# A spacer of 448 bytes, value products in two runs and query turns of 128 columns in a hybrid attention trunk

## The chip, the cores and the metric

The kernel runs on one core of a Trainium2 chip. The metric is device time in microseconds of one execution, as the median of several runs. TensorE (PE in the rows) does the matmuls and, in a queue of its own (PEld), loads the stationary operand; VectorE is DVE, ScalarE is ACT, GpSimd is POOL, and SyncE (SP) issues the transfers.

## The reference, cut to what matters

Two layers act on 1024 latent and 256 context tokens of width 1024. In each, a normalised input goes through one input projection and from there into three parallel mixers (a spatial gating MLP, a windowed attention with 8 query and 2 key heads, a linear recurrence), whose outputs meet in one output projection; then comes a gated FFN of width 2816. The attention, to which most of the change belongs:

```python
s_loc = jnp.einsum('bnqhgd,bnkhd->bnhgqk', qb, kw).astype(jnp.float32) * scale
s_ctx = jnp.einsum('bnqhgd,bchd->bnhgqc', qb, kc).astype(jnp.float32) * scale
...
p = jax.nn.softmax(jnp.concatenate([sink_l, s_ctx, s_loc], axis=-1), axis=-1)
...
o = jnp.einsum('bnhgqc,bchd->bnqhgd', p_ctx, vc) + jnp.einsum('bnhgqk,bnkhd->bnqhgd', p_loc, vw)
```

A query tile of 128 tokens sees the two context tiles and up to three latent tiles, so it has 2 (context queries), 4 (the first and the last latent tile) or 5 key tiles. The FFN is `(silu(gu[..., :D_FF]) * gu[..., D_FF:]) @ w_down` with `gu = h @ w_gu`.

## The kernel before, in words

**Memory.** SBUF is cut into four pools in this order: constants, the weight pool (`wts`), small statistics (`stats`, from `small`), and 33 equal slots of 128 x 1280 float32 (5120 bytes of each partition) that `alloc` hands out and `rel` takes back in turn. Every large tile that isn't a weight lies in a slot: the activations `h`, `q` and `qs`, `P`, `PT`, `Vt`, `ah` and `al`. The weight buffers are 4096 bytes each and start at byte 25344 of a partition, the slots at byte 59712. Some weights of the out-projection and one pair of the FFN are put in slots too; in the rows they are `wsh` and `wsl` instead of `wh` and `wl`.

**Matmuls.** `mm` (L145) issues one, and so every matmul has line 145. `mm3` makes a product of two numbers that are each split in a high and a low part: high by high, high by low, low by high, as three matmuls. In the rows `dd<-h,wh` reads: output tile `dd` in PSUM, moving operand `h`, stationary operand `wh`; `128*128` is the part of the array that is used (rows by columns), and `128x512` is the moving operand. Operands of type float32 (in transposes and in `pv`) leave two rows per matmul where the others leave one; transposes of P and q come as four rows for a group of four by the names of this trace.

**Attention.** A unit is a query tile and one of two head groups: 20 units in layer 0 and 16 in layer 1. Four generators work at once on different units: `q_proj(n+2)` projects the queries (24 matmuls `mm<-wh,h` and `mm<-wl,h`), `a_q(n+1)` turns them (four transposes by the identity in `cst_sb`) and splits them into `qs`, `a_s(n)` computes scores (`dd<-kh,qs`, `dd<-kl,qs`) and the softmax `P`, and `a_o(n-1)` turns each 128 x 128 block of `P` and multiplies it by the values. A string of letters says whose turn it is, step by step (one step is the code up to the next `yield`):

```python
for z in "spspspspqopopsopopooos":
```

Between the steps a background list puts in small matmuls of the next stage (`xx<-jT`, 32 x 32). In `a_o` the turned blocks of key tile j go to PSUM, are copied to `PT` by ScalarE (even j, L1144) or VectorE (odd j, L1146), and `pv(j)` multiplies them: two matmuls `xx<-PT,Vt`, one for each half of the output partitions, with 64 stationary columns. Before the change pv(j-2) follows the transposes of block j, and the last two come one step apart after all blocks.

**FFN.** For each of 22 slices of 128 channels `gate_up` makes gate and up (`dd<-h,wh`: h moves, the weights are stationary) in groups of 512 or 256 tokens, and `ffn_down` adds the product with `w_down` (`mm<-wh,ah` and `xx<-wh,ah`: the weights move in 512 columns, the activation is stationary).

Of the kernel before, what the change touches and what calls it, by code (L numbers as in the profile page):

```python
# [10 lines left out]
F32 = mybir.dt.float32  # L11
# [80 lines left out]
def trunk(ctx: ExitStack, tc: tile.TileContext, x, ctxt, cc, w_mod, pp, w_in, w_out, lng, lnb, sgw, sink,  # L92
          w2, a2, g2, w_gu, w_down, cst, rope, out, dbg=None):
    nc = tc.nc
    V, S, G, T, D = nc.vector, nc.scalar, nc.gpsimd, nc.tensor, nc.sync
# [3 lines left out]
    stp = ctx.enter_context(tc.tile_pool(name="stats", bufs=4))  # L99
# [10 lines left out]
    def alloc(name, dt=F32):  # L110
        i = free.popleft()
        return Slot(sp.tile([128, NTOK], dt, tag=f"s{i}", name=nm(name)), i)

    def rel(*ss):
        for s in ss:
            free.append(s.i)
# [13 lines left out]
    def mm_t():  # L130
        return p_t("gg", 1) if psum["units"] else p_t("mm", 2)

    def x_t():
        return p_t("gg", 1) if psum["units"] else p_t("xx", 2)
# [9 lines left out]
    def mm(o, lhsT, rhs, start=True, stop=True):  # L144
        T.matmul(o, lhsT=lhsT, rhs=rhs, start=start, stop=stop)  # L145

    def mm3(o, a, b, start, stop):
        mm(o, a[0], b[0], start, False)
        mm(o, a[0], b[1], False, False)
        mm(o, a[1], b[0], False, stop)  # L150


    K = cp.tile([128, CSTW], F32, name="cst_sb")
    PP = cp.tile([128, L * PPW], F32, name="pp_sb")
    cs_ = alloc("silu")
# [2 lines left out]
    D.dma_start(PP, pp)  # L158
    ident = K[:, C_ID:C_ID + 128]
    blk = K[:, C_BLK:C_BLK + 128]  # L160
    mLK = K[:, C_LK:C_LK + 128]
    mG = K[:, C_G:C_G + 128]
    mF = K[:, C_F:C_F + 64]
    I2 = K[:, C_I2:C_I2 + 64]
    hs = K[:, C_HS:C_HS + 2]
# [68 lines left out]
    def wget(ahead=2, slots=False):  # L234
        if not ready:
            emit_w(slots)
        r = ready.popleft()
        while len(ready) < ahead and plan:
            emit_w(slots)
        return r  # L240
# [212 lines left out]
    def hk(hT, k, c0, n):  # L453
        if c0 < 256:
            return tuple(hT[z][k].t[:, 1024 + c0:1024 + c0 + n] for z in range(2))
        z = 0 if c0 >= 768 else 1
        o = c0 - (768 if z == 0 else 256)
        return tuple(hT[z][k].t[:, o + j:o + j + n] for j in (0, 512))
# [98 lines left out]
    def layer(l):  # L557
# [345 lines left out]
        for name in ("v", "u"):  # L903
# [3 lines left out]
            for t0 in range(0 if full else 2, NT, 2):  # L907
                ps = mm_t()
# [56 lines left out]
        def rot(ps, o, nh, n, tmp):  # L965

            hv = [128, nh, 64]
            v3 = lambda ap: ap.rearrange("p (h d) -> p h d", d=64)
            V.tensor_tensor(v3(o), v3(ps), rt4[:, 0, n:n + 1, :].to_broadcast(hv), op=ALU.mult)
            V.tensor_tensor(v3(tmp), v3(ps), rt4[:, 1, n:n + 1, :].to_broadcast(hv), op=ALU.mult)  # L970
            v4 = lambda ap: ap.rearrange("p (a b f) -> p a b f", b=2, f=16)
            G.tensor_tensor(v4(o), v4(o), v4(tmp)[:, :, ::-1, :], op=ALU.add)
# [5 lines left out]
        for t0 in range(0, NT, 2):  # L978
            ps = mm_t()
            for j in range(2):  # L980
                proj256((wA, wB), t0 + j, ps[:, j * 256:(j + 1) * 256])
            pv = ps.rearrange("p (j c) -> p j c", j=2)
# [45 lines left out]
        def a_geo(t):  # L1028
            if t < 2:
                return 0, 0, [0, 1]  # L1030
            lo = max(2, t - 1)
            hi = min(NT - 1, t + 1)
            return lo * 128, (hi - lo + 1) * 128, list(range(lo, hi + 1)) + [0, 1]
# [2 lines left out]
        wq, sst = {}, {}  # L1036
        QQ, QS = alloc("q"), alloc("qs", F32R)

        def q_proj(n):
            t, g = units[n]  # L1040
            if t == tiles_q[0]:
                wq[0] = wget(), wget()
            ps = mm_t()
            for k in range(8):
                wt = wq[0][k // 4]
                c = (k % 4) * 256
                mm3(ps[:, 0:256], hk(hT, k, t * 128, 128), (wt[0][:, c:c + 256], wt[1][:, c:c + 256]), k == 0, k == 7)
                if k < 7:
                    yield
            q = QQ.t[:, n % 2 * 640:n % 2 * 640 + 512]  # L1050
            if t < 2:
                S.activation(q[:, 0:256], ps[:, 0:256], AF.Copy)
            else:
                rot(ps[:, 0:256], q[:, 0:256], 4, t - 2, q[:, 256:512])

        def a_q(n):
            q = QQ.t[:, n % 2 * 640:n % 2 * 640 + 512]
            ps = x_t()
            for h in range(4):
                T.transpose(ps[0:64, h * 128:(h + 1) * 128], q[:, h * 64:(h + 1) * 64], ident)  # L1060
            s = QS.t[:, n % 2 * 640:n % 2 * 640 + 512]
            S.activation(s[0:64], ps[0:64, :], AF.Copy)
            V.tensor_tensor(s[64:128], ps[0:64, :], s[0:64].bitcast(F32), op=ALU.subtract)
# [55 lines left out]
        def a_o(n):  # L1119

            t, g = units[n]
            keys = a_geo(t)[2]
            P = sst.pop(n)
            PT = []
            po = x_t()

            def pv(j):
                for e in range(2):
                    c = (j % 2) * 512 + e * 256
                    mm(po[64 * e:64 * e + 64, 0:256], Vt.t[:, keys[j] * 128 + g * 64:keys[j] * 128 + g * 64 + 64],  # L1130
                       PT[j // 2].t[:, c:c + 256], j == 0, j == len(keys) - 1)
                if j % 2 or j == len(keys) - 1:
                    rel(PT[j // 2])
            for j in range(len(keys)):
                ps = x_t() if j % 2 else mm_t()
                for i in range(4):
                    c = (i % 2) * 640 + j * 128
                    z = (i % 2) * 2 + i // 2
                    T.transpose(ps[:, z * 128:(z + 1) * 128], P[i // 2].t[:, c:c + 128], ident)
                if j % 2 == 0:  # L1140
                    PT.append(alloc("PT"))
                o = PT[j // 2].t[:, (j % 2) * 512:(j % 2) * 512 + 512]
                if j % 2 == 0:
                    S.activation(o, ps, AF.Copy)  # L1144
                else:
                    V.tensor_copy(o, ps)  # L1146
                if j == len(keys) - 1:
                    rel(*P)
                if j >= 2:
                    pv(j - 2)  # L1150
                yield
            pv(len(keys) - 2)
            yield
            pv(len(keys) - 1)
            yield
            ot = alloc("attO")
            S.activation(ot.t[:, 0:256], po[:, 0:256], AF.Copy)
            D.dma_start(od[t][:, 256 + g * 256:512 + g * 256], ot.t[:, 0:256])
            rel(ot)
# [197 lines left out]

        N = len(units)
        weave(q_proj(0), k_turn(0))
        run(q_proj(1))  # L1360
        a_q(0)
        bs_ = beta_start()
        for n in range(N + 1):
            gs = {"s": a_s(n) if n < N else iter(()), "o": a_o(n - 1) if n else iter(()),
                  "p": q_proj(n + 2) if n + 2 < N else bs_}
            for z in "spspspspqopopsopopooos":
                if z != "q":
                    next(gs[z], None)
                elif n + 1 < N:
                    a_q(n + 1)  # L1370
            if n == N // 2 - 2:
                bgq.appendleft(k_turn(1))
            bg(BG_A)
            bg(EL_A, 1)
            if n == N // 2 - 2:
                while len(khh) < 2 or not rw.get('kt'):
                    bg(1)
            for z in "pos" if n + 2 < N or n == N else "os":
                run(gs[z])
            if n == N - 3:  # L1380
                rel(rt, *hT[0], *hT[1])
# [295 lines left out]
    for l in range(L):  # L1677
        layer(l)
# [33 lines left out]
```

## Time and profile before

| what | value |
|---|---|
| median of 3 runs | 3435.76 us (3434.49 to 3438.95) |
| the profiled execution | 3435.06 us |
| its span in the trace | 3433.3 us |
| TensorE busy | 3310.5 us (96%) |
| VectorE, ScalarE, GpSimd busy | 1789.0, 1256.5, 331.6 us (52%, 37%, 10%) |

The span is the time from the first to the last record; the execution's own time is 1.8 us longer. Busy shares are means over the program. Layer 0 has its attention at 376 to 585 us and its FFN at 950 to 1870 us; layer 1 has them at 2203 to 2400 and 2690 to 3433 us.

### The profile page before, as it was taken

The numbers are of one execution on the slowest core, as the hardware profiler recorded it, in microseconds if no ns is written. First come the engines' busy times: TensorE is split into PE (matmuls) and PEld (weight loads), VectorE is DVE, ScalarE is ACT, GpSimd is POOL, SyncE is SP. The second block draws the span as 40 slices with busy tenths as digits, with TensorE's granted clock in tenths as the row PEclk, the third lists the DMA queues.
The fourth block names the chain that finished last, engine by engine and source line by source line (L and its number), as shares of the span: only waits on it lengthen the run. The fifth ranks groups of instructions, "written<-read, shape, count | busy, mean of one in ns | idle before, by whom it ended". The sixth has DMA issues, their size and how long they took to land. (4 is left out here: it accounts for less than half of the span.)

```text
span 3433.3 us, 51729 instructions
## 1 busy us (share of the span) xinstructions
PE 3310.5 (96%) x20348; PEld 2646.9 (77%) x20348; DVE 1789.0 (52%) x3747; ACT 1256.5 (37%) x2735; POOL 331.6 (10%) x460
## 2 busy tenths in 40 slices
PE   7998999999999999999999998999999999999998
PEld 4777877777787777778888777877777788888887
DVE  3458778775523333333334658878674433433445
ACT  4354476663431111111113554466663411111112
POOL 2103101231100000000001202111121000000000
PEclk9998999999999999999999998999999999999999
DMA  5784212546312222221113375323445111111113
GB/s 205 235 251 141 76 59 68 141 135 221 130 46 72 80 86 80 73 69 62 37 37 107 110 236 162 114 63 89 111 143 190 56 43 44 49 49 50 49 41 119
DMA packets 381779, 354.40 MB, mean 103 GB/s; under 512 B 111968, under 2 KB 332768, under 8 KB 381536
## 3 DMA queue, kind: packets, MB, share of 16 engines
q1 hardware_dynamic: 381536, 351.09, 32.7%
q8 instruction: 161, 2.64, 0.3%
q14 instruction: 82, 0.67, 0.1%
HBM read 255.20 MB, written 95.81 MB: 102 GB/s over the span
## 5 line engine op out<-in xcount | busy, mean ns | idle before, releaser
L145 PE MATMUL dd<-h,wh 128*128 128x512 f32 (+1 forms) x3440 | 992.3, 373 | 2.6 <-DVE h L436 2.3
L145 PEld LDWEIGHTS dd<-h,wh 128*128 128x128 f32 x3440 | 624.8, 189 | 147.0 <-issue 30.2
L145 PE MATMUL dd<-h,wl 128*128 128x512 f32 (+1 forms) x1720 | 637.7, 371 | 0.0
L228 ACT ACTIVATE wh<-wr 128x1024 fp32r<-128x1024 f32 x172 | 180.7, 1058 | 694.3 <-PE xx L145 379.1
L229 DVE TENSOR_TENSOR wl<-wr,wh 128x1024 fp32r<-128x1024 f32 x172 | 209.4, 1225 | 348.6 <-ACT wh L228 344.1
L145 PEld LDWEIGHTS dd<-h,wl 128*128 128x128 f32 x1720 | 325.0, 189 | 62.9 <-issue 5.0
L145 PE MATMUL mm<-wh,h 128*128 128x256 f32 x1472 | 320.6, 295 | 1.9 <-ACT gel L913 1.4
L1514 DVE SCALAR_TENSOR_TENSOR ft<-ft,dd 128x512 f32<-128x512 f32 (+1 forms) x110 | 69.5, 632 | 459.6 <-ACT ft L1513 459.6
L145 PEld LDWEIGHTS mm<-wh,h 128*128 128x128 f32 x1472 | 247.7, 194 | 29.2 <-issue 26.5
L1513 ACT ACTIVATE ft<-dd 128x512 f32<-128x512 f32 (+1 forms) x110 | 60.5, 550 | 502.2 <-PE dd L145 501.6
L145 PE MATMUL mm<-h,wh 128*128 128x512 f32 (+1 forms) x816 | 234.6, 372 | 1.5 <-ACT ntmp L428 0.7
L176 POOL TENSOR_TENSOR ss<-ss,mh_sb 128x1 f32<-128x1 f32 x74 | 50.4, 682 | 1856.7 <-DVE ss L405 1850.4
L145 PE MATMUL mm<-wl,h 128*128 128x256 f32 x736 | 211.0, 287 | 4.9 <-DVE wl L229 4.9
L145 PEld LDWEIGHTS mm<-h,wh 128*128 128x128 f32 x816 | 145.5, 193 | 35.5 <-issue 10.8
L1545 DVE TENSOR_TENSOR yac<-yac,mm 128x512 f32<-128x512 f32 x180 | 123.4, 686 | 95.0 <-PE mm L145 94.8
L1545 DVE TENSOR_TENSOR yac<-yac,xx 128x512 f32<-128x512 f32 x180 | 123.5, 686 | 90.0 <-PE xx L145 90.0
L145 PE MATMUL mm<-wh,ah 128*128 128x512 f32 x396 | 157.1, 397 | 1.9 <-DVE yac L1545 1.8
L145 PE MATMUL xx<-wh,ah 128*128 128x512 f32 x396 | 157.0, 396 | 0.0
L145 PE MATMUL xx<-wl,ah 128*128 128x512 f32 x396 | 156.7, 396 | 0.0
L145 PE MATMUL mm<-wh,al 128*128 128x512 f32 x396 | 156.5, 395 | 0.0
L145 PE MATMUL xx<-wh,al 128*128 128x512 f32 x396 | 156.5, 395 | 0.0
L145 PE MATMUL mm<-wl,ah 128*128 128x512 f32 x396 | 156.5, 395 | 0.0
(315 smaller groups left out, 5965.8 us busy)
## 6 DMA issues: line engine op xcount, KB each, us to landing
wr<-in_w_gu SPq DMA_DIRECT2D x88, 512.0 KB, 3.7
wm<-in_w_mod SPq DMA_DIRECT2D x80, 512.0 KB, 4.5
wr<-in_w_down SPq DMA_DIRECT2D x44, 512.0 KB, 3.3
wr<-in_w_in SPq DMA_DIRECT2D x38, 512.0 KB, 4.8
cb<-ao SPq DMA_DIRECT2D x76, 256.0 KB, 3.0
ao<-rk SPq DMA_DIRECT2D x58, 256.0 KB, 4.1
xs<-xr SPq DMA_DIRECT2D x28, 512.0 KB, 2.8
xr<-xs SPq DMA_DIRECT2D x26, 512.0 KB, 4.3
```

Source lines behind the costliest of these rows:

```text
L145: T.matmul(o, lhsT=lhsT, rhs=rhs, start=start, stop=stop)
L176: G.tensor_tensor(dst, src, mh[:, :n], op=ALU.pow)
L228: S.activation(hi, raw, AF.Copy)
L229: V.tensor_tensor(lo, raw, hi.bitcast(F32), op=ALU.subtract)
L1513: S.activation(tm, ps[:, 0:n], AF.Tanh, scale=0.5)
L1514: V.scalar_tensor_tensor(tm, tm, 1.0, ps[:, 0:n], op0=ALU.add, op1=ALU.mult)
L1545: V.tensor_tensor(yac[t].t[:, c], yac[t].t[:, c], ps, op=ALU.add)
```

## The change

It has four edits. A tile of 112 float32 (448 bytes) that nobody uses is put at the start of the stats pool, so that every later tile of this pool and all slots start 448 bytes further: the slots at byte 60160 instead of 59712, the weights where they were. Per layer, two strips of 64 columns in the q tile are cleared on GpSimd. `a_q` turns 128 columns at a time, the head and what lies behind it, onto 128 partitions of PSUM, of which the upper 64 are not read; the cleared strip is what lies behind the last head of a unit. And `a_o` multiplies in two runs: for five key tiles pv(0) and pv(1) behind the transposes of block 3 and the rest behind the last block, one step later; for four or two key tiles all of them there.

```diff
+    stp.tile([128, 112], F32, name="gap", bufs=1)
     K = cp.tile([128, CSTW], F32, name="cst_sb")
...
         QQ, QS = alloc("q"), alloc("qs", F32R)
 
+        for z in range(2):
+            G.memset(QQ.t[:, z * 640 + 256:z * 640 + 320], 0.0)
+
         def q_proj(n):
...
             for h in range(4):
-                T.transpose(ps[0:64, h * 128:(h + 1) * 128], q[:, h * 64:(h + 1) * 64], ident)
+                T.transpose(ps[:, h * 128:(h + 1) * 128], q[:, h * 64:h * 64 + 128], ident)
...
                 if j == len(keys) - 1:
                     rel(*P)
-                if j >= 2:
-                    pv(j - 2)
+                if j == 3 and len(keys) == 5:
+                    pv(0)
+                    pv(1)
                 yield
-            pv(len(keys) - 2)
-            yield
-            pv(len(keys) - 1)
+            yield
+            for j in range(2 if len(keys) == 5 else 0, len(keys)):
+                pv(j)
             yield
```

The lines behind the first edit are numbered one higher after the change, those behind the second four higher. The diff doesn't show what the engines' orders become, so here are three pieces of them.

TensorE in the attention of layer 0, a unit with five key tiles, before; `mm<-cst_sb,P` and `xx<-cst_sb,P` are transposes of P, two from each of its two tiles, and a row with x2 behind `PT,Vt` is one key tile:

```order
L1139 MATMUL mm_4069<-cst_sb,P_3838 128x128 x2
L145 MATMUL xx_4038<-PT_4044,Vt_3013 64x256 x2
...
L1139 MATMUL xx_4081<-cst_sb,P_3838 128x128 x2
L145 MATMUL xx_4038<-PT_4044,Vt_3013 64x256 x2
...
L145 MATMUL xx_4114<-jT_3705 32x32 x13
...
L1139 MATMUL mm_4095<-cst_sb,P_3838 128x128 x2
L145 MATMUL xx_4038<-PT_4074,Vt_3013 64x256 x4
L145 MATMUL xx_4114<-jT_3705 32x32 x7
L145 MATMUL dd_4178<-kh_3434,qs_3417 128x256
L145 MATMUL xx_4038<-PT_4100,Vt_3013 64x256 x2
```

The same unit in the changed kernel:

```order
L1143 MATMUL mm_4072<-cst_sb,P_3841 128x128 x2
L145 MATMUL mm_4003<-wh_3010,h_234 128x256
...
L1143 MATMUL xx_4082<-cst_sb,P_3841 128x128 x2
L145 MATMUL xx_4041<-PT_4047,Vt_3014 64x256 x4
...
L145 MATMUL xx_4117<-jT_3708 32x32 x17
...
L1143 MATMUL mm_4098<-cst_sb,P_3841 128x128 x2
L145 MATMUL xx_4041<-PT_4077,Vt_3014 64x256 x4
L145 MATMUL xx_4117<-jT_3708 32x32 x3
L145 MATMUL dd_4181<-kh_3437,qs_3418 128x384
L145 MATMUL dd_4181<-kh_3437,qs_3418 128x256
L145 MATMUL xx_4041<-PT_4103,Vt_3014 64x256 x2
```

Four runs of pv became three: the first two key tiles now go together behind the fourth block. Over both layers TensorE's order has 115 runs of these matmuls before and 75 after, with 320 matmuls in both.

GpSimd in layer 0, from the gating MLP (`gel`) to the attention, after the change; `q` is the tile whose strips are cleared, `kt` the keys whose rotation GpSimd finishes:

```order
L916 TENSOR_SCALAR gel_2994<-gel_2994 128x512
L1041 MEMSET q_3417 128x64 x2
L973 TENSOR_TENSOR kt_3015<-kt_3015,rtmp_3149 128x128 x2
L973 TENSOR_TENSOR kt_3015<-kt_3015,rtmp_3251 128x128 x2
L973 TENSOR_TENSOR kt_3015<-kt_3015,rtmp_3343 128x128 x2
```

The two clears were not there before; the rest is in the same order.

## Rows read from the trace of the kernel before

**Rows 1.** Windows: stretch, length, busy us of each engine, granted clock, DMA share, GB/s.

```profile
376.00:585.00 209.00, 205.85 (x1931) 165.96 (x1929) 167.05 (x464) 144.31 (x334) 25.42 (x44) 1.00 0.22 62
...
2360.00:2400.00 40.00, 33.77 (x312) 23.36 (x306) 32.34 (x90) 27.83 (x60) 7.48 (x15) 1.00 0.39 119
```

**Rows 2.** Timeline of TensorE, attention of layer 0: start, length, operation.

```profile
417.59 0.60 PE L1139 MATMUL xx<-cst_sb,P 128*128 128x128 f32 x4
417.94 0.37 PE L145 MATMUL mm<-wh,h 128*128 128x256 f32 x1
...
418.38 0.60 PE L1139 MATMUL mm<-cst_sb,P 128*128 128x128 f32 x4
418.91 0.65 PE L145 MATMUL xx<-PT,Vt 128*64 128x256 f32 x4
419.49 0.38 PE L145 MATMUL mm<-wh,h 128*128 128x256 f32 x1
...
422.92 1.08 PE L145 MATMUL xx<-PT,Vt 128*64 128x256 f32 x8
423.94 0.43 PE L145 MATMUL xx<-jT 32*32 32x32 f32 x14
```

**Rows 3.** Groups by line; the second is of the attention of layer 0 alone.

```profile
L145 PE MATMUL xx<-PT,Vt 128*64 128x256 f32 x640 | 96.2, 399 | 4.5 <-DVE qs L1063 2.2 <-ACT PT L1144 1.7 <-DVE PT L1146 0.3
...
L1144 ACT ACTIVATE PT<-mm 128x512 f32<-128x512 f32 x43 | 25.3, 588 | 7.4 <-PE mm L1139 5.9 <-ACT PT L1144 0.8 <-ACT wh L228 0.5
```

**Rows 4.** Timeline of the weight loads, attention of layer 0.

```profile
429.60 0.43 PEld L1060 LDWEIGHTS xx<-cst_sb,q 128*64 128x64 f32 x4
430.03 0.47 PEld L1139 LDWEIGHTS mm<-cst_sb,P 128*128 128x128 f32 x4
430.46 0.19 PEld L145 LDWEIGHTS mm<-wh,h 128*128 128x128 f32 x1
```

**Rows 5.** Timeline of GpSimd ahead of the attention of layer 0; idle time before in brackets.

```profile
361.84 1.05 POOL L972 TENSOR_TENSOR kt<-kt,rtmp 128x128 f32<-128x128 f32 x2 [9.28 <-DVE rtmp L970]
```

**Rows 6.** Timeline of TensorE, FFN of layer 0.

```profile
970.31 0.62 PE L145 MATMUL dd<-h,wh 128*128 128x512 f32 x2
...
975.80 0.61 PE L145 MATMUL dd<-h,wsh 128*128 128x512 f32 x2
...
976.49 0.61 PE L145 MATMUL dd<-h,wsh 128*128 128x512 f32 x2
...
981.25 0.39 PE L145 MATMUL mm<-wh,ah 128*128 128x512 f32 x1
```

**Rows 7.** The chain that ended last, FFN of layer 1: start, length, what.

```profile
2741.84 44.80 PE dd L145 x192
2786.63 1.40 PE mm L145 x6
...
2809.03 43.96 PE dd L145 x192
```

**Rows 8.** Groups by line and shape: count, busy us, mean ns.

```profile
L145 PE MATMUL dd<-h,wh 128*128 128x512 f32 x2752 | 864.2, 395 | 0.3 <-POOL h L436 0.3
...
L145 PE MATMUL mm<-wh,h 128*128 128x256 f32 x1472 | 320.6, 295 | 1.9 <-ACT gel L913 1.4 <-DVE rtmp L970 0.5
...
L145 PE MATMUL mm<-h,wh 128*128 128x512 f32 x576 | 187.5, 404 | 0.4 <-ACT raw L825 0.2
L145 PE MATMUL mm<-wh,ah 128*128 128x512 f32 x396 | 157.1, 397 | 1.9 <-DVE yac L1545 1.8
...
L145 PE MATMUL dd<-h,wh 128*128 128x256 f32 x688 | 129.0, 286 | 2.3 <-DVE h L436 2.3
```

**Rows 9.** Timeline of TensorE, FFN of layer 0, matmuls of 256 columns.

```profile
928.85 0.40 PE L145 MATMUL dd<-h,wh 128*128 128x256 f32 x2
...
930.97 0.40 PE L145 MATMUL dd<-h,wsh 128*128 128x256 f32 x2
...
933.84 0.62 PE L145 MATMUL dd<-h,wh 128*128 128x512 f32 x2
```

## The prediction, made before the change was run

> **What bounds the kernel now.** I read the windows first, stage by stage, because an average over the program hides which engine ends the waits. In the attention of layer 0 TensorE is busy 205.85 of 209 us at a granted clock of 1.00, VectorE 167.05 and ScalarE 144.31 [rows 1]. Then I followed the chain that ended last through the FFN of layer 1: it is made of TensorE's blocks, one behind the other [rows 7], and the FFN is the longest stage in both layers. So in these stages a nanosecond that leaves TensorE's stream leaves the program, one that is added lengthens it, and work that is added on another engine costs nothing as long as it fits its gaps. The one part that is not so tight is the end of the layer-1 attention: 33.77 of 40 us [rows 1].
>
> Since TensorE is the bound, its busy total says nothing more. What counts is the distance from the start of one matmul to the start of the next, since matmuls overlap and the duration of one is longer than that step. The timeline gives start times, and all prices below are differences of those.
>
> **Part 1: fewer runs of pv.** Take two places in one unit. Without a pv run, four transposes of P begin at 417.59 and the next projection matmul at 417.94: 0.35 us. With a run of four pv rows between (one key tile; each pv matmul leaves two rows), transposes at 418.38, pv at 418.91, projection at 419.49: 1.11 us [rows 2]. So the run costs 0.76 us. How much of it is the pv work? A run of eight, two key tiles, takes 422.92 to 423.94, 1.02 us, and the run of four 0.58 us, so four rows more cost 0.44 us [rows 2]. The other 0.76 - 0.44 = 0.32 us are the price of going in and out: 0.18 in (0.53 from the transposes to pv against 0.35 to a projection) and 0.14 out.
>
> "TensorEngine Tiling (Array Packing)" of the Trainium skill, under Key Properties, says that a change of tiling mode, and not a change of tile alone, drains the engine. The pv matmuls have the tile 128*64 and their neighbours 128*128 or 32*32, so the 0.32 us would be such drains by that rule. But it would say the same of the query turns, which are 128*64 too before the change; that is weighed in part 2.
>
> The same 640 pv rows [rows 3] stand in TensorE's order in 115 runs before and in 75 after: 40 runs fewer, 40 x 0.32 = **-12.8 us**. Bounds: if only the way in is saved, 40 x 0.18 = -7; the upper one is the whole of it at 0.34, -14 (start times are rounded to 0.01). I take the whole, because the run of eight shows that longer runs pay in and out once.
>
> What does it take away? Before, a pv run stood between two groups of transposes and gave the copy of a transposed block (588 ns on ScalarE, [rows 3]) time to end. Where projection matmuls of a later unit stand between, they still do. The last units of each layer have none left to project: three or so a layer, and there a wait of up to 0.59 us can open. I take 6 x 0.33 = **+2 us**. The last pv of a five-key unit reads the block that was transposed just before; ahead of it the order keeps a pv run of two key tiles (1.02 us), three small matmuls and two scores matmuls, more than the 0.59 us of the copy, so I cost it at nothing; uncovered it would cost the 0.59 us.
>
> **Part 2: the 128-column query turns and the two clears.** Turns are a transpose by an identity with q as the stationary operand. The weight loads of four turns of 64 columns begin at 429.60, of four P turns of 128 columns at 430.03, and of the next projection at 430.46: 0.43 us each [rows 4]. A turn of 128 columns takes the step of one of 64, so 36 units save and lose **0**. The columns that are new hold the next head or the cleared strip and land on partitions 64 to 127 of the PSUM tile, which nothing reads.
>
> The rule on modes just named would have the turns drain as well, at most the 0.32 us of a pv run each, 36 x 0.32 = 11.5 us saved. This case's rows speak against it: the step into P from the turns is no longer than inside them [rows 4]. That result is the last rival below.
>
> The clears are two per layer on GpSimd. In layer 0 they stand ahead of the additions to kt; such a pair takes 1.05 us and GpSimd has been waiting 9.28 us for VectorE before it [rows 5]. Two clears of 64 columns, bounded by that pair, fit. What is queued behind them is kt, which the key turns wait for, so if a clear waited long for the last reader of its slot, kt would be late by that. The slot's tile was a value tile whose readers are done before that stage; I take **0**, at worst the 1 us of a pair per layer.
>
> **Part 3: the spacer.** It does no work. It moves every tile of the stats pool and of the slots by 448 bytes, and the weight pool not at all. Before, weight buffers start 256 bytes over a multiple of 512 and slots 320 over; after, both 256. So the question is whether TensorE's step depends on where its two operands lie. Three pairs can be compared at 512 columns.
> - Both in slots: 24 matmuls of h and wsh/wsl from 975.80 to 981.25, 5.45 us, 227.1 ns each; the first three are slower, and the other 21, from 976.49 on, take 4.76 us, 226.7 ns [rows 6]. I take 226.7.
> - Moving h in a slot, stationary weights in the weight pool, same tile, just before: 970.31 to 975.80, 5.49 us [rows 6], 228.8 ns. In layer 1 blocks of 192 take 43.96 and 44.80 us in turn [rows 7]: 229.0 and 233.3 ns with the same tiles.
> - Moving weights in the weight pool, stationary ah in a slot (ffn_down): 6 in 1.40 us [rows 7], 233.3 ns.
>
> Clock and neighbours are the same, so the place of the operands is left as what differs, and after the change every pair has the relation that slots have among themselves. If that relation sets the step, all go to 226.7:
> - gate and up, layer 1: 2752 + 1376 (the hi-lo third) matmuls of 512 columns over both layers [rows 8], some 10.5 blocks of 192 in layer 1. Against 43.53 a block, (0.43 + 1.27) / 2 = 0.85 saved, **-8.9**; layer 0, 2112 steps by 2.1 ns, **-4.4**.
> - ffn_down: 6 groups of 396 [rows 8] by 6.6 ns, **-15.7**.
> - input projections, 576 and half as many again [rows 8], priced like gate and up, 864 x 2.2 = **-1.9**.
>
> Matmuls of 256 columns go the other way: 18 with weights in the weight pool take 928.85 to 930.97, 117.8 ns each, and 24 with both in slots 930.97 to 933.84, 119.6 ns [rows 9]. The 688 + 344 of the FFN and 1472 + 736 of the projections [rows 8], 3240 x 1.8 = **+5.8**. The sum of part 3 is -30.9 + 5.8 = **-25.1 us**. Bounds: -31 if 256 columns lose nothing, and 0 if the place means nothing.
>
> Against it stands "TensorE: Matmul & The Clock Gate" of the Trainium skill, Part 2, Step-by-step: TensorE has two independent read ports to SBUF, so that loading the next weights takes no bandwidth from the matmul that runs. By that rule the place of one operand relative to the other is worth 0. The rows have 228.8 against 226.7 ns in neighbouring blocks [rows 6], which that rule doesn't explain; it is the first rival.
>
> **Sum.** The profiled execution took 3435.06 us (0.7 below the median 3435.76): 3435.1 - 12.8 + 2 - 25.1 = 3399.2, and 0.7 more for the median: **3400 us**.
>
> **Rivals.**
> - *The spacer does nothing.* The slower step belongs to the pool, the buffers' use or the kind of operand (what is weight, what is activation), not to the byte offset. For it: blocks of 229.0 and 233.3 ns with the same tiles [rows 7], so something other than the place counts too. Against it: in both cases the pair of different pools is slower. Then only the runs of pv count: 3435.8 - 10.8 = 3425 us.
> - *Slower: the offset of the weight pool is the bad one.* If a step is slow because an operand starts 256 over 512, and slots were fast because they did not, the spacer takes every 512-column step to 233.3 ns: layer 0 2112 x 4.5 = 9.5, layer 1 5.25 blocks x 0.84 = 4.4, input projections 864 x 4.5 = 3.9, and the out-projection from slots some more: at least +17.8. With the runs, 3443 us or a little above. It decides from 10.8 us on, where it eats the gain of the runs, and is measurably slower from about 17.7. For it: ffn_down, whose moving operand lies there, is the slowest pair. Against: gate and up in layer 1 have both rates with the same buffers.
> - *The longer runs are paid for by new waits.* If the last pv of a unit waits for its copy, 0.30 us in each of 36 units eats the 10.8 us; the copy is 0.59. For it: the thin end at 2360 to 2400 us [rows 1]. Against: the order keeps 1.02 us of pv and five matmuls ahead. 3411 us with the spacer's gain, 3436 without.
> - *The turns were draining* (the rule above): 11.5 more, 3388 us.
>
> **How the numbers follow.** Chances: forecast 0.53, spacer null 0.22, slower spacer 0.11, new waits 0.11 (0.07 with, 0.04 without the spacer's gain), turns 0.03. A measurement of this kernel can tell about 0.2%, 6.9 us, from no change. Faster: 0.53 + 0.22 + 0.07 + 0.03, less a little for a spacer null with waits in part, 0.81; within: the rest of the waits and the lower half of the slower case, 0.09; slower 0.10. The forecast's own range is 3390 to 3412. The range goes from 3382 (turns and no loss at 256 columns) to 3432, which takes in the null spacer with the runs at their lower bound, and leaves out the slower spacer and the waits without a gain, 0.15, and a few hundredths below.
>
> **What would show it.** Right: ffn_down's six matmuls in 1.36 us instead of 1.40; blocks of 192 all near 43.5; a group of 18 at 256 columns near 2.15; 75 runs of pv in TensorE's rows; no row of TensorE waiting on PT by more than 1 us outside the ends of the attention. Wrong: ffn_down still at 1.40 (first rival), gate and up all at 44.8 (second), or an attention stage that is not 5 us shorter per layer though its runs are fewer (third).

## The result, and the profile after the change

The changed kernel takes 3392.73 us (median of 4 runs, 3389.75 to 3394.0), the kernel before 3435.12 us in the runs beside it. The ratio is 0.9875, with a 95% interval of 0.9858 to 0.9892: 42 us faster, where 35.8 were forecast. The span of the profiled execution falls from 3433.3 to 3390.7 us.

The page and, below it, the chain that ended last in the FFN of layer 1 (start, length, what), which answers to [rows 7]:

```profile
PE 3274.7 (97%) x20348; PEld 2659.0 (78%) x20348; DVE 1787.4 (53%) x3747; ACT 1254.8 (37%) x2735; POOL 330.9 (10%) x464
```

```profile
2713.81 43.52 PE dd L145 x192
2757.33 1.36 PE mm L145 x6
...
2779.09 43.52 PE dd L145 x192
```

TensorE has lost 36 us of busy time with the same number of rows. Blocks of 192 that took 43.96 and 44.80 us in turn all take 43.52, and six ffn_down matmuls 1.36 instead of 1.40: 226.7 ns a step in both. The timeline of TensorE in the FFN of layer 0, matmuls of 512 columns first, then those of 256, answers to [rows 6, 9]:

```profile
965.35 0.62 PE L145 MATMUL dd<-h,wh 128*128 128x512 f32 x2
...
970.79 0.62 PE L145 MATMUL dd<-h,wsh 128*128 128x512 f32 x2
...
976.23 0.39 PE L145 MATMUL mm<-wh,ah 128*128 128x512 f32 x1
```

```profile
924.08 0.40 PE L145 MATMUL dd<-h,wh 128*128 128x256 f32 x2
...
926.23 0.40 PE L145 MATMUL dd<-h,wsh 128*128 128x256 f32 x2
```

Weights from the weight pool and weights from slots now take the same: 24 matmuls in 5.44 us each, 965.35 to 970.79 and 970.79 to 976.23. At 256 columns 18 matmuls take 2.15 us instead of 2.12; that is the small loss that was forecast.

The timeline of the attention of layer 0, first TensorE, then the weight loads of the query turns, then GpSimd ahead of the attention; they answer to [rows 2, 4, 5]:

```profile
420.16 0.60 PE L1143 MATMUL mm<-cst_sb,P 128*128 128x128 f32 x4
420.51 0.36 PE L145 MATMUL mm<-wh,h 128*128 128x256 f32 x1
...
420.95 0.60 PE L1143 MATMUL xx<-cst_sb,P 128*128 128x128 f32 x4
421.48 1.08 PE L145 MATMUL xx<-PT,Vt 128*64 128x256 f32 x8
422.50 0.39 PE L145 MATMUL mm<-wh,h 128*128 128x256 f32 x1
```

```profile
398.42 0.46 PEld L1064 LDWEIGHTS xx<-cst_sb,q 128*128 128x128 f32 x4
398.85 0.47 PEld L1143 LDWEIGHTS mm<-cst_sb,P 128*128 128x128 f32 x4
399.28 0.19 PEld L145 LDWEIGHTS mm<-wh,h 128*128 128x128 f32 x1
```

```profile
344.44 0.23 POOL L1041 MEMSET q<- 128x64 f32 x2 [4.07 <-PE dd L145]
353.83 0.86 POOL L973 TENSOR_TENSOR kt<-kt,rtmp 128x128 f32<-128x128 f32 x2 [9.16 <-DVE rtmp L971]
```

One run for two key tiles costs (422.50 - 420.95) - (420.51 - 420.16) = 1.20 us, of which 0.88 is pv work: again 0.32 at its ends. The wide turns are 0.43 us apart as before. The clears take 0.23 us in a gap, and GpSimd still waits 9.16 us behind them.

Where the time went, stage by stage, from the start of the first matmul of one stage to that of the next in the two timelines:

| stage | before | after | difference |
|---|---|---|---|
| attention, layer 0 | 213.5 | 208.5 | -5.0 |
| attention, layer 1 | 193.0 | 182.6 | -10.4 |
| FFN, layer 0 | 994.5 | 984.0 | -10.5 |
| FFN, layer 1 | 742.5 | 725.0 | -17.5 |
| out-projections | 226.1 | 224.3 | -1.9 |
| input projections | 644.3 | 646.4 | +2.1 |
| start and scans | 407.6 | 407.5 | -0.1 |

Single profiles differ by some 3 us in a stage with many transfers (the input projections above all, where the granted clock in layer 0 is 0.92 in the profile before and 0.91 in the one after), so the small rows of the table say little. For the two attention stages the windows split the time into TensorE's busy time and the rest; in the order before and after for layer 0, then for layer 1:

```profile
382.74:596.22 213.48, 210.31 (x1946) 166.28 (x1946) 167.35 (x462) 148.97 (x345) 25.56 (x44) 0.99 0.21 58
385.32:593.85 208.53, 203.01 (x1945) 168.01 (x1945) 165.79 (x462) 148.41 (x345) 24.84 (x44) 0.99 0.22 60
2205.87:2398.89 193.02, 184.54 (x1738) 143.42 (x1735) 155.56 (x419) 130.60 (x286) 23.48 (x40) 0.99 0.23 65
2190.82:2373.40 182.58, 177.07 (x1738) 144.73 (x1736) 153.72 (x419) 130.21 (x286) 23.92 (x41) 0.99 0.25 71
```

The busy time falls alike in both, by 7.3 and 7.5 us, while the time in which TensorE idles rises from 3.2 to 5.5 us in layer 0 and falls from 8.5 to 5.5 in layer 1.

### The profile page after: what moved, and what is told of

It reads as the page before. It is cut to its first block, busy times and chain, and to the rows that moved or that the text cites. A ratio compares the mean times of both kernels' runs of the same rounds, so it can differ in the third digit from the quotient of the medians.

```text
span 3390.7 us, 51725 instructions
## 1 busy us (share of the span) xinstructions
PE 3274.7 (97%) x20348; PEld 2659.0 (78%) x20348; DVE 1787.4 (53%) x3747; ACT 1254.8 (37%) x2735; POOL 330.9 (10%) x464
## 5 line engine op out<-in xcount | busy, mean ns | idle before, releaser
L145 PE MATMUL mm<-wh,h 128*128 128x256 f32 x1472 | 327.6, 299 | 0.0
```

## The experiments

There are twelve kernels. Each is compared with runs of the kernel before on the same chip, whose median there is 3430 to 3434 us.

**The parts alone.** The spacer on the kernel before:

```diff
+    stp.tile([128, 112], F32, name="gap", bufs=1)
     K = cp.tile([128, CSTW], F32, name="cst_sb")
```

> The spacer alone. Theory (the step of a matmul depends on where its two operands lie relative to each other): FFN blocks of 192 at 43.5 us and six ffn_down matmuls at 1.36 as in the changed kernel, the FFN stages 28 us shorter, projections and attention 2 to 4 us longer for the 256-column steps: 3435 - 25 = about 3410 us. Rival (the shorter FFN of the changed kernel came with the new order and not with the bytes): 3435 us with blocks of 43.96 and 44.80 as before.

It took 3400.59 us beside 3430.92, ratio 0.9909 (0.9896 to 0.9922). The chain in the FFN of layer 1:

```profile
2721.40 43.52 PE dd L145 x192
2764.92 1.36 PE mm L145 x6
```

The theory holds, with more gain than it gave: the bytes alone change the step, while the kernel's instructions and their work are those of before. The two FFN stages are 31 us shorter in this one profile.

The two runs alone (the `a_o` of the change, in the kernel before):

> The two-run attention alone, with turns of 64 columns and no spacer. Theory: 40 runs fewer at 0.32 us, -12.8 us, and the end of the layer-1 attention, which got shorter and not longer in the changed kernel, another -3 to -5: 3418 to 3422 us. Rival (the shorter end comes from the 128-column turns): -10 to -13, 3422 to 3425 us with the waits on PT before 2400 us still there.

3418.32 us, ratio 0.9963 (0.9951 to 0.9975): 12.6 us. Its blocks in the FFN stay at the old step, as the chain shows:

```profile
2728.53 44.80 PE dd L145 x192
2773.32 1.40 PE mm L145 x6
```

The attention stages are 4.5 and 10.7 us shorter, nearly what they are in the changed kernel, so the surplus in layer 1 belongs to the order of pv and not to the wide turns.

The turns and the clears alone:

> The 128-column turns and the clears alone. Theory: 0, 3435 us, and loads of four turns still 0.43 us apart. Rival (turns of 64 columns drain the array as the runs of pv do): 36 units at up to 0.32 us, -11.5, 3423 us.

3433.03 us, ratio 1.0002 (0.9994 to 1.0011). No gain and no loss; the rival falls.

Spacer and runs without the turns (the changed kernel with the old transposes and no clears):

```diff
-                T.transpose(ps[:, h * 128:(h + 1) * 128], q[:, h * 64:h * 64 + 128], ident)
+                T.transpose(ps[0:64, h * 128:(h + 1) * 128], q[:, h * 64:(h + 1) * 64], ident)
```

> Spacer and two-run attention together, without turns and clears. Theory: the same as the changed kernel, 3392 to 3394 us, the sum of the two parts measured alone. Rival (the turns carry part of the gain, or the parts need each other): 3397 to 3405 us.

3389.45 us, ratio 0.9876 (0.9862 to 0.989), the same as the changed kernel. And 0.9909 x 0.9963 = 0.9872: the two parts add up and don't need each other.

**What about the bytes?** Three other spacers, and one move of both pools together, in the changed kernel. The distance is that of the slots' start from the weight buffers', counted up to 256 bytes.

```diff
-    stp.tile([128, 112], F32, name="gap", bufs=1)
+    stp.tile([128, 16], F32, name="gap", bufs=1)
```

That one has 64 bytes; the other two have 48 and 96 float32, 192 and 384 bytes. For the move of both, a tile of 16 float32 stands in the pool of constants, ahead of the weight pool.

> The changed kernel with a spacer of 64 bytes: slots at 59776, 384 over a multiple of 512, weight buffers at 256 over, so 128 apart. Theory in its wide form (the two operands must lie alike up to 512 bytes): not helped, gate and up between 43.9 and 44.8 us a block and ffn_down at 1.40, about 3418 to 3422 us. Narrow form (alike up to 128 bytes is enough): the same as with 448, 3392 us, blocks 43.5 and 1.36.

> The changed kernel with a spacer of 192 bytes: slots at 59904, a multiple of 512, weight buffers 256 over. Wide form: not helped, 3418 to 3422 us. Alike up to 128 or 256 bytes is enough: 3392 us, blocks 43.5 and 1.36.

> The changed kernel with 64 bytes more ahead of the weight pool: weight buffers and slots both 320 over a multiple of 512, where the slots lay before. Theory (only the place of one operand relative to the other counts): the same as the changed kernel, 3392 us, blocks 43.5 and 1.36. Rival (the fast place is 256 over 512, or a multiple of 128, for each operand by itself): blocks of 44 and more, 1.40, 3415 us or longer.

> The changed kernel with a spacer of 384 bytes: slots 192 over a multiple of 512, weight buffers 256 over, so 64 apart as before the change but on the other side. Theory after the runs with 64 and 192 bytes (alike up to 256 bytes is fast, all else is slow): gate and up at 43.9 to 44.8 us a block, ffn_down at 1.40, 3416 to 3429 us. Rival (only one sign of the distance costs): 3392 us, blocks 43.5 and 1.36.

| kernel | weights over 512 | slots over 512 | distance up to 256 | us | ratio to before (95%) | block of 192, layer 1 |
|---|---|---|---|---|---|---|
| two runs alone, no spacer | 256 | 320 | 64 | 3418.32 | 0.9963 (0.9951 to 0.9975) | 43.96 and 44.80 |
| 64 bytes | 256 | 384 | 128 | 3429.2 | 0.9987 (0.9978 to 0.9997) | 44.80 |
| 384 bytes | 256 | 192 | 192 | 3424.83 | 0.9981 (0.9972 to 0.999) | 44.80 |
| 192 bytes | 256 | 0 | 0 | 3391.26 | 0.9882 (0.9868 to 0.9897) | 43.52 |
| 448 bytes (the change) | 256 | 256 | 0 | 3392.73 | 0.9875 (0.9858 to 0.9892) | 43.52 |
| 448 and both moved by 64 | 320 | 320 | 0 | 3391.0 | 0.9881 (0.9867 to 0.9896) | 43.52 |

The chain of three of them, 64, 384 and 192 bytes in this order:

```profile
2734.97 44.80 PE dd L145 x192
2779.76 1.40 PE mm L145 x6
...
2802.16 44.80 PE dd L145 x192
```

```profile
2771.52 1.40 PE mm L145 x6
...
2791.12 44.80 PE dd L145 x192
...
2838.68 1.37 PE mm L145 x6
...
2841.43 1.37 PE mm L145 x6
```

```profile
2713.23 43.52 PE dd L145 x192
2756.75 1.36 PE mm L145 x6
```

The reader is to see that the blocks that alternate at a distance of 64 are all at the slow step at 128 and at 192, and all at the fast one at 0, wherever that 0 lies. With 384 bytes it is ffn_down that alternates, 1.40 and 1.37 us for six (233.3 and about 229 ns), so the 1.40 that I expected there holds for every other group only. The two kinds of matmul agree if the distance is counted from the stationary to the moving operand: gate and up move a slot and ffn_down a weight buffer, so they are 64 and 192 apart before the change, and 192 and 64 with 384 bytes. At 64 both steps occur, at 128 and 192 the slow one, at 0 the fast one. The offset 320, at which the slots lay before, is as good as 256 when the weights share it; so 256 is no special place for an operand by itself. The slower rival of the prediction (the weight pool's own place is the bad one) had fallen with the changed kernel's own blocks. The wide form of the theory falls too, since 256 apart is as good as 0 apart, and so does the narrow one, since 128 apart is slow. What counts in these runs is that the two operands lie alike up to 256 bytes.

**What a run's ends cost.** The pv matmuls over 128 stationary columns instead of 64, so that the array's tile does not change; half of the output partitions hold the other head group and are not read:

```diff
-                for e in range(2):
-                    c = (j % 2) * 512 + e * 256
-                    mm(po[64 * e:64 * e + 64, 0:256], Vt.t[:, keys[j] * 128 + g * 64:keys[j] * 128 + g * 64 + 64],
-                       PT[j // 2].t[:, c:c + 256], j == 0, j == len(keys) - 1)
+                c = (j % 2) * 512
+                mm(po, Vt.t[:, keys[j] * 128:keys[j] * 128 + 128], PT[j // 2].t[:, c:c + 512], j == 0, j == len(keys) - 1)
```

> The changed kernel with value products over 128 stationary columns: both head groups' values are the stationary operand, one matmul of 512 columns for a key tile in place of two of 256, half of the output partitions is not used, and ScalarE copies the output in two pieces. Theory (the 0.32 us at a run's ends is the change between the tile 128*64 and 128*128): the 75 runs that are left lose it, -24 us, about 3368 us, with the pv work itself unchanged at 0.44 us a key tile. Rival (the price belongs to the float32 operands or to the wait for the copied block): 3390 to 3394 us.

3441.42 us, ratio 1.0025 (1.0015 to 1.0035): 1.5% longer than the changed kernel and not 24 us shorter. The timeline, a run for two key tiles, and the group of these matmuls:

```profile
423.71 0.60 PE L1141 MATMUL xx<-cst_sb,P 128*128 128x128 f32 x4
424.15 1.88 PE L145 MATMUL xx<-PT,Vt 128*128 128x512 f32 x4
425.47 0.68 PE L145 MATMUL mm<-wh,h 128*128 128x256 f32 x1
425.99 0.28 PE L145 MATMUL mm<-wl,h 128*128 128x256 f32 x1
```

```profile
L145 PE MATMUL xx<-PT,Vt 128*128 128x512 f32 x320 | 149.7, 599 | 2.9 <-ACT PT L1146 2.0 <-DVE qs L1067 0.5
```

Two things are in these rows. The ends did get cheap: from the transposes to pv 0.44 us instead of 0.53, and from pv to the second projection matmul 1.84 us, which is four rows at 0.43 and the 0.12 of an ordinary step. That is the theory. But a key tile now takes 0.86 us and not 0.44 [rows 2]: the two halves of 64 columns had been running side by side (the two matmuls of a pair start within 0.01 us of each other in the trace), and one matmul over all 128 columns can't. 160 key tiles by 0.42 are 67 us more; the attention stages grew by 24.5 and 22.2, 46.7 us, so about 20 us of it were given back, against 24 by 75 runs of 0.32. Some 3 us of the 20 may be the clock: the changed kernel's profile has 3.41 us at half clock in each of the two stages, this one none. The part of the expectation that left the work unchanged was wrong, the part on the ends is borne out in the rows and roughly in size. "TensorEngine Tiling (Array Packing)" of the Trainium skill, Key Properties, states both halves: a change of mode drains the array, and different tiles run in parallel. For pv the rows agree with both. For the query turns, 128*64 as well, they don't: they paid nothing for the change, and what sets them apart was not tried. They use one half of the columns where pv uses both, and the wide pv gave up the second half together with the tile, so it can't tell which of the two costs.

**Fewer runs still.** The block of the fifth key tile goes into the free ends of the two PT tiles (256 columns each, copied by ScalarE and by VectorE), so that a third slot isn't needed and all products of a unit follow the last block:

```diff
-                if j == 3 and len(keys) == 5:
-                    pv(0)
-                    pv(1)
...
-            for j in range(2 if len(keys) == 5 else 0, len(keys)):
+            for j in range(len(keys)):
                 pv(j)
```

> The changed kernel with the fifth key tile's block in the free ends of the two PT tiles, its two halves copied by ScalarE and VectorE, and all value products of a unit issued after the last block. TensorE's order then has 65 runs of pv instead of 75. Theory: 10 x 0.32 us less, 3388 to 3391 us, just at the edge of what can be measured. Rival (holding back the first products leaves the transposes waiting for their copies again): 3394 us or more, with waits on PT.

3393.02 us, ratio 0.989 (0.9873 to 0.9906), no gain that can be told. Among TensorE's waits in the attention of layer 0 (us in total, times, longest) are two for copies of blocks, by ScalarE:

```profile
PE xx L145 <- ACT PT L1153: 1.0, 1, 1.0
...
PE xx L145 <- ACT PT L1148: 0.7, 2, 0.3
```

The attention stages are 1.3 and 1.9 us longer than in the changed kernel. The order has only ten runs fewer, and 13 of the 65 hold a single matmul, which has no neighbour to run beside. No version here beats the changed kernel by more than can be measured.

**Where the surplus in layer 1 lies.** The attention of layer 1 gained about 5 us more than its runs explain. In the trace before there is a place at which a pv waits 2.19 us behind a clear of the next stage on VectorE. I took it for a wait for the pv's copy; the rows, from the timeline of all engines, name the split of the queries (`qs`) instead, and VectorE's copy begins only 0.02 us before the pv:

```profile
2376.88 0.91 DVE L1171 MEMSET bC<- 128x1024 f32 x1 [2.11 <-DMA od<-attO]
...
2377.82 0.69 DVE L1063 TENSOR_TENSOR qs<-xx,qs 64x512 fp32r<-64x512 f32 x1
2378.54 0.69 DVE L1146 COPY PT<-xx 128x512 f32<-128x512 f32 x1
2378.56 0.65 PE L145 MATMUL xx<-PT,Vt 128*64 128x256 f32 x4 [2.19 <-DVE qs L1063]
```

So I split the two-run order by units, in the kernel before:

```diff
+            two = n >= len(units) - 3
...
+                if two and j == 3 and len(keys) == 5:
+                    pv(0)
+                    pv(1)
+                if not two and j >= 2:
+                    pv(j - 2)
```

and the other way round with `n < len(units) - 3`.

> The kernel before with the two-run attention in the last three units of each layer alone, where no query projection is left to stand between; 108 runs of pv in TensorE's order instead of 115. Theory (the forecast missed the end of the layer-1 attention, where a pv used to wait for its copy): 7 x 0.32 = 2.2 us and about 5 us of waits less, the layer-1 attention at 187 to 188 us instead of 193, in all 3424 to 3428 where before is 3431. Rival (the extra gain lies in the middle units): the layer-1 attention at 191 to 193 us, 2 us less in all.

> The kernel before with the two-run attention in all units but the last three of each layer; 82 runs of pv instead of 115. Theory: 33 x 0.32 = 10.6 us less and the waits at the end as before, layer-1 attention at 187 to 188 us, layer-0 attention at 208 to 209, 3420 us where before is 3431. Rival (the extra gain lies in the middle units): layer-1 attention at 183 to 184 us, 3416 us.

The end alone: 3436.33 us, ratio 1.0015 (1.0006 to 1.0023), the layer-1 attention at 192.7 us. All but the end: 3424.03 us, ratio 0.9975 (0.9966 to 0.9984), the layer-1 attention at 184.2 us. My theory of the end falls: the two-run order in the last three units gains next to nothing, and the surplus comes with the order of the units before them. But some of it is waits at the end even so. In the last 44 us of the stage TensorE's listed waits add up to 6.0 us before, 5.9 with the end alone and 3.0 with all but the end, whose last units have the old order. With the spacer alone, the old order throughout, they are 4.1 us, so they differ between profiles too.

Both kernels give some of the gain back behind the attention of layer 0, where the scan stage takes 195.1 and 194.1 us against 189.8. The windows of that stage, before and with all but the end, and a piece of the latter show why:

```profile
596.22:786.02 189.80, 184.88 (x1856) 139.37 (x1855) 137.05 (x449) 132.01 (x454) 54.59 (x66) 1.00 0.50 143
597.30:791.40 194.10, 190.30 (x1859) 142.79 (x1858) 137.68 (x450) 131.72 (x453) 53.69 (x66) 0.96 0.48 141
718.54:728.78 10.24, 10.24 (x55) 7.33 (x54) 4.85 (x14) 4.70 (x16) 3.49 (x5) 0.50 0.09 20
```

TensorE idles no longer there than before (4.4 and 3.8 us against 4.9). Its granted clock is lower, 0.97 (599.21 to 794.31, the end alone) and 0.96 against 1.00: in both there is a stretch of 10.24 us at the lower of its two levels, 1.2 instead of 2.4 GHz, into which TensorE went while busy. So the totals say less here than the stages.

The starts of the turns of two units, four units apart, in the timeline before and in that of all but the end:

```profile
2270.08 0.27 PE L1060 MATMUL xx<-cst_sb,q 128*64 128x128 f32 x1
...
2324.51 0.60 PE L1060 MATMUL xx<-cst_sb,q 128*64 128x128 f32 x4
```

```profile
2269.68 0.60 PE L1060 MATMUL xx<-cst_sb,q 128*64 128x128 f32 x4
...
2319.67 0.60 PE L1060 MATMUL xx<-cst_sb,q 128*64 128x128 f32 x4
```

54.4 us against 50.0 around the change from the first head group to the second. Between them the timeline has 15 runs of pv before and 9 in the other, 6 x 0.32 = 1.9 us. Most of the other 2.5 us is the clock: the window before holds 3.41 us at 0.50, soon after a wait of 1.01 us for a copy, and the other window holds none. (With the spacer alone the same wait, 0.97 us, stands there and the clock doesn't fall, so what makes it fall is not shown.)

```profile
2270.08:2324.51 54.43, 52.94 (x577) 41.69 (x575) 34.56 (x89) 35.36 (x80) 6.70 (x12) 0.97 0.25 62
2285.59:2289.00 3.41, 3.41 (x51) 3.12 (x51) 1.12 (x2) 1.81 (x5) 0.00 (x0) 0.50 0.00 0
...
2269.68:2319.67 49.99, 48.16 (x573) 39.49 (x572) 35.49 (x96) 35.16 (x80) 6.18 (x12) 1.00 0.29 77
```

Half of 3.41 us is 1.7, and 0.8 us stay open. The clock also explains why the stage is not the same in every kernel with the old order in most units (190.1 to 195.6 us over four of them): the shortest has no time at half clock in it and the longest 10.2 us. With half of such time taken off, an estimate, the four come to 190.1 to 191.3 us, and the seven with the change's order of pv in all units to 180.6 to 181.5. So the gain in layer 1 is 9 to 10 us, of which 20 runs at 0.32 are 6.4.

## Why the prediction was right, step by step

**The FFN term.** Forecast -8.9, -4.4 and -15.7, with +1.9 at 256 columns, -27.1 us in all; the two stages lost 28.0, some 2 of them by the clock (13.9 us at 0.50 in these stages before, 9.4 after). The step of 226.7 ns that was taken from 21 matmuls with both operands in slots is the step of the FFN's 512-column matmuls afterwards, blocks of 192 and groups of six alike. The rule of two independent read ports ("TensorE: Matmul & The Clock Gate", Part 2, of the Trainium skill) does not account for these runs: moving one operand's pool by bytes moved the step by 3%. The whole of part 3 was -25.1, bounds -31 and 0; the spacer alone gave 30.3 us, 27 to 36 by its interval. What was left out, the out-projections, gave 1.9 us in the changed kernel.

**The runs of pv.** The mechanism was right: the price lies at a run's ends and goes with the tile 128*64 as pv uses it, as the wide pv shows. It was a little small. In each layer the traces have 20 runs fewer, -6.4; with +0.9 for 480 steps of 256 columns in layer 0 and +0.7 in layer 1 that is -5.5 and -5.7. TensorE's busy time fell by 7.3 and 7.5, which is 0.41 us a run once the loss at 256 columns is added back. Measured by the stages it is -5.0 and -10.4; the difference between the layers is idle time of TensorE, +2.3 in one and -3.0 in the other, so that layer 0 came out near its forecast is in part luck.

**The step that failed** is the +2 us for waits at the units without a projection. Over both attention stages TensorE's idle time fell by 0.7 us: in the last 44 us of the stage the listed waits fell from 6.0 to 3.0 in layer 1 and rose from 2.4 to 3.1 in layer 0, and the rest of layer 0's rise lies in the middle of its stage. This term (2.7 us) and the price that was too small (14.8 us of busy time, where 12.8 less the 1.6 at 256 columns were forecast) make 6.3 of the 6.6 us between forecast and result. The order of the last units, which I suspected next, is not what shortened the end of layer 1; why the idle time moved one way in one layer and the other way in the other stays open.

**The turns and the clears** are worth nothing, alone or together with the rest, for the reason given: a turn of 128 columns has the step of one of 64.

**The rivals.** New waits of pv for the copies did not come: TensorE's idle time ahead of pv fell from 4.5 us [rows 3] to 1.0, as the group of the changed kernel shows, and no wait on `PT` in its attention stages is longer than 0.8 us.

```profile
L145 PE MATMUL xx<-PT,Vt 128*64 128x256 f32 x640 | 87.0, 396 | 1.0 <-ACT PT L1148 0.3
```

The slower spacer is decided by the blocks of the changed kernel, the null spacer and the draining turns by the parts alone.

## What to carry to other kernels

Where TensorE is the bound, compare the start-to-start step of equal matmuls whose operands lie in different pools before anything else: here 3% of the step hung on 64 bytes, a tile that nobody uses gave it back, and both distances tried that are a multiple of 256 bytes did. Group the matmuls that use another tile of the array, since a visit can cost at its ends (pv paid, the query turns did not). But keep pairs of half-width tiles paired: they ran side by side, and that was worth more than all visits together. And before the time of a stage in a single profile is explained by the order of its instructions, look at the granted clock in it.

## What the runs showed of the hardware that was not expected

- The step of a 512-column matmul in the FFN is 226.7 ns with operands a multiple of 256 bytes apart (three placements of the pools). Counted from the stationary to the moving operand up to 256, it is 233.3 at 128 and at 192; at 64 it is about 229 or 233.3 in alternate blocks of layer 1, for gate and up before the change and for ffn_down with 384 bytes. What chooses between the two was not found.
- Two float32 matmuls of 256 columns on the two 64-column halves of the array take 0.44 us for two passes each, one of 512 columns over the whole width 0.86.
- A turn on the tile 128*64 pays nothing at its ends; a run of pv on the same tile pays 0.32 us where two places are compared, 0.41 by the fall of TensorE's busy time over 20 runs in each layer.
